# Linear-attention heads beside matrix products: keys stacked on the chip, scores a chunk ahead, wider decay steps

## The chip, the cores and the metric

The kernel runs on one core of a Trainium2 chip. Its time is the device time of one launch in microseconds (us), as the median of several runs. A core has five engines with instruction queues of their own, each in order: TensorE (PE, matrix products and transposes), VectorE (DVE), ScalarE (ACT), GpSimd (POOL) and SyncE (SP). SP and POOL issue the DMAs here.

## The reference, cut to what matters

A streaming encoder step with two layers, stick-breaking attention first and gated linear attention (GLA) second, for 512 prompt frames and 8 running streams of 16 new frames each (640 rows, width 2048). The change lies mostly in the GLA layer, which has 4 heads with 256 key and 512 value columns:

```python
def gla_chunk(S, inp):
    """S_t = diag(a_t) S_{t-1} + k_t^T v_t, o_t = q_t S_t; g = log a_t."""
    q, k, v, g = inp
    b = jnp.cumsum(g, axis=1)
    b_last = b[:, -1]
    q_in = q * jnp.exp(b)
    a = jnp.einsum('bchd,bshd->bhcs', q_in, k * jnp.exp(-b))
    a = jnp.where(jnp.tril(jnp.ones((C, C), dtype=bool)), a, 0.0)
    o = jnp.einsum('bhcs,bshe->bche', a, v) + jnp.einsum('bchd,bhde->bche', q_in, S)
    S = jnp.exp(b_last)[..., None] * S + jnp.einsum('bshd,bshe->bhde', k * jnp.exp(b_last[:, None] - b), v)
    return S, o
...
    g = log_sigmoid(a_lr @ w_a2 + b_a) / GLA_TAU          # the decays
    S, o = lax.scan(gla_chunk, S0, ...)
    o = o * lax.rsqrt(jnp.mean(o * o, axis=-1, keepdims=True) + EPS) * g_out
    y = (o * silu(r)) @ w_out
```

The prompt starts from a state of zeros; each of the 8 streams has a state of its own, read from and written to DRAM (256 x 512 numbers a head and stream).

## The kernel before, in words

Products keep nearly full precision with 32-bit operands split into a high and a low part (`halves`: a cast on ACT, a subtraction on DVE) and three products for one. The first 957 us hold the modulation (`six`) and the projections of layer 0 by seven products where eight would do (`by_sevens`); then the attention of layer 0 with plain and shared products beside it, up to 1538 us; queries and the seven-products of layer 1, up to 2072 us. Then comes the stage that the change is about, the heads' stage, to 2496 us, and the final products (L356 and L1746).

In the heads' stage PE works on a stream of large products, the fill: first `others` (L1314), the projections of q and k of heads 2 and 3 by `plain` (320 columns each, L575), then `share` for two groups of output rows (512 columns, L619). Between pieces of the fill the planner `Side` slips in steps of four lanes. A lane is a generator; `yield step(wait, tp, z)` says after how much of PE's work, on the planner's own count `pe["now"]`, its next step may come, and how many PSUM banks it takes. This fixes the order on PE. The instructions of the other engines follow from the code by a scheduler, and each engine's queue is in order.

- `decays` (L1396) makes a head's decays: the products of `alr_in` and `wa` (L1423), then ACT and DVE over 640 columns (Abs, Exp, Ln, a scan at L1429), and scales q and k in place by exponentials (L1445, L1446) by halves of the 640 columns, for the two halves `dt` of the 256 key columns. `wa` comes from six small loads `wa2r`. Heads 2 and 3 wait for all of `others`.
- `prompt_lane` (L1450) goes through 4 heads of 4 chunks: scores (`attend`, L1356), keys transposed (L1499) into `krh` and `krl`, the state as `S1h` and `S1l` (L1471, L1472), the output by `mm3` (L1344), `normed` (L1364, with a reciprocal root `on_r` on POOL at L230), and the state's update (L1525, L1527). `leave` (L1384) transposes the normalised rows (L1388), multiplies by the gate (L1389) and stores them as `og`; the gate of a later chunk is loaded into that buffer afterwards.
- `sample_lane` (L1556) does the 8 streams, 4 at a time in four groups a head (`e` for which of two streams, `dt`). A group multiplies the queries `qz` by four states (L1612, into the bank `z`), then updates each state by a product of the stacked keys `kst` and values `vst` (L1618) and DVE (L1620), and the state is stored (`leaves`) and, 8 us of PE work later, the next one asked into its buffer (`ask`). There are `S0` = 8 such buffers. `kst` holds high, high and low rows of the keys of four streams. They get there through DRAM: two transposes (L1584), `krh` and `krl` stored to `st_d`, and six loads for each `stack(e, dt)`, all on POOL's queue:

```python
def stack(e, dt):
    for i in range(3):
        rows = st_d[h][int(i == 2)][:, P * dt:P * dt + P].rearrange("(m e t) n -> e t m n", m=4, e=2)[e]
        r0 = 64 * e + NT * i
        move(kst[e][r0:r0 + NT].bitcast(F32), rows)
```

- `fetches` (L1630) loads rows `kt` of `og` (two buffers, tag `pl`, which the projections use too) and splits them into `ogh` and `ogl` for the fill. `share` starts when the four rows of its group are there (`side.until`, L1670). Rows 14 and 15 are loaded in the final stage.

Of the kernel before, what the change touches and what calls it, by code (L numbers as in the profile page):

```python
# [15 lines left out]
P = 128  # L16
# [17 lines left out]
S0 = 8  # L34
# [7 lines left out]
def hybrid_step_kernel(ctx: ExitStack, tc: tile.TileContext, A: dict, O: list):  # L42
# [77 lines left out]
    st_d = [[dp.tile([P, 256], F32, name=f"k_{h}_{d}") for d in range(2)] for h in range(GH)]  # L120
# [33 lines left out]

    def wpiece(src, a, n):

        return [t.rearrange("p (a n) -> p a n", a=a) for t in split(wraw(src, a, n))]
# [276 lines left out]
    def six(h, w, n0, acc, until, asked):  # L434
# [4 lines left out]
        def piece(j):  # L439
            asked()  # L440
            return wpiece(src[:, j:j + 9:8, n0:n0 + 512], 2, 512)

        nxt = piece(0)
        yield
        for j in range(8):
            until(j)
            wh, wl = nxt
            if j < 7:
                nxt = piece(j + 1)
# [107 lines left out]
    def plain(h, src, parts):  # L557
# [3 lines left out]
        def piece(n):  # L561
            if n < len(todo):
                n0, k0, _ = todo[n]
                return wpiece(src[:, k0:k0 + 8, n0:n0 + P], 8, P)

        nxt, acc = piece(0), None
        for n, (n0, k0, leave) in enumerate(todo):
# [3 lines left out]
            for nt in range(2):  # L571
# [33 lines left out]
    def share(g, og, w, leave=None, at=None, first=None):  # L605
# [30 lines left out]
        for c in range(4):  # L636
            ws = [w0, w1]
            if c < 3:
                raws += [raw(c + 1, 0), raw(c + 1, 1)]
                w0 = made()  # L640
# [3 lines left out]
            for a in each:  # L644
# [3 lines left out]
                leave(a, c, acc)  # L648
            if len(each) == 3:
# [648 lines left out]
    with tc.tile_pool(name="gl", bufs=1, reuse_waits="tile") as gl:  # L1298
        came = {"plain": False, "last": False}

        def keep(dst, hh):
            t = []

            def leave(nt, pt):
# [4 lines left out]
                if nt:  # L1309
                    move(dst[:, hh, :], t[0])  # L1310
            return leave
# [3 lines left out]
                                 for n0, dst in ((256 * h, gq_d[h]), (NK + 256 * h, gk_d[h])) for hh in range(2)])  # L1315
# [35 lines left out]
        def attend(t0, kT, qT):  # L1351
# [8 lines left out]
            parts = [gl.tile([P, P], F32R, tag=n, name=n, bufs=2) for n in ("aTh", "aTl")]  # L1360
# [3 lines left out]
        def normed(o):  # L1364
# [4 lines left out]
            r = rstd_of(gl, s1, 512, "on")  # L1369
# [26 lines left out]
        def decays():  # L1396

            for h in range(GH):
                while min(through.values()) < h - 1 or h >= 2 and not came["plain"]:
                    yield step(0.5)  # L1400
                q, k = (gl.tile([P, 2, T], F32, tag=n, name=n, bufs=2) for n in ("q", "k"))
                r = gl.tile([96, 256], F32, tag="e", name="wa2r", bufs=1)
                for n in range(6):
                    load(r[16 * n:16 * n + 16, :], A["gla_w_a2"][0][:, 256 * h:256 * h + 256])
                load(q, gq_d[h])
                load(k, gk_d[h])
# [3 lines left out]
                dve.tensor_tensor(wa2[64:96, :], r[64:96, :], wa2[64:96, :].bitcast(F32), op=ALU.subtract)  # L1410

                e1, el, ed = (gl.tile([P, 2, 4], F32, tag=n, name=n, bufs=2) for n in ("e1", "el", "ed"))
                es = gl.tile([P, 2, NB], F32, tag="es", name="es", bufs=2)
                yield step(5.0)
                for dt in range(2):
# [3 lines left out]
                    for c in hs:  # L1419
# [5 lines left out]
                        dve.tensor_scalar(y[:, c], pt, ba, 0.0, op0=ALU.add, op1=ALU.min)  # L1425
                    act(b, b, AF.Exp, scale=-1.0)
                    act(b, b, AF.Ln, bias=1.0)
                    dve.tensor_tensor(y, y, b, op=ALU.subtract)
                    dve.tensor_tensor_scan(b, reset, y, 0.0, ALU.mult, ALU.add)  # L1429
                    bp = b[:, :NP].rearrange("p (c t) -> p c t", t=P)  # L1430
# [6 lines left out]
                    act(ed[:, dt], ed[:, dt], AF.Exp, scale=IT)  # L1437
                    act(es[:, dt], bs[:, :, 15:16].rearrange("p c o -> p (c o)"), AF.Exp, scale=IT)
                    m = gl.tile([P, 4], F32, tag="m", name="m")
                    dve.tensor_copy(m, b1)  # L1440
                    dve.tensor_tensor(bp, bp, m.unsqueeze(2).to_broadcast([P, 4, P]), op=ALU.subtract)
                    for x, sign, f in ((q, 1.0, 1.0 / 16.0), (k, -1.0, 1.0)):
# [7 lines left out]
        def prompt_lane():  # L1450
# [25 lines left out]
            def leave_left():  # L1476
# [3 lines left out]
                if c == 3:  # L1480
                    through["p"] = h + 1
# [293 lines left out]
```

## Time and profile before

| | us |
|---|---|
| median of 3 runs | 2615.43 (2614.98 to 2615.93) |
| the profiled execution | 2618.87, span 2617.2 |
| PE busy in the span | 2448.4 (94%) |
| DVE, ACT, POOL busy | 1601.5, 1021.0, 259.5 |
| mean granted clock of PE | 0.971 of full speed |

The profile is of one execution. An engine's busy time is the time in which one of its instructions ran; a row of the trace gives an instruction's start and length, and in brackets how long the engine had been idle and what released it. Matrix products are pipelined: a product of 320 columns shows some 0.31 us, while the next one starts after about half of that. The granted clock is the share of full speed that PE was given, 1.00 for 2.4 GHz. A wait "issue" is one for which the profile shows no releaser.

### The profile page before, as it was taken

To read this page: it belongs to the slowest core of one execution; us is meant where nothing else is said; L and a number is where in the kernel's file an instruction comes from. 1 tells how busy PE (TensorE), PEld (TensorE's weight loads), DVE (VectorE), ACT (ScalarE), POOL (GpSimd) and SP (SyncE) were. 2 spreads that over 40 slices of the span, in tenths; PEclk is the share of its full clock that TensorE was granted. 3 is DMA by queue.
4 is the path that set the end of the run, shared out by engine and by line. 5 is a ranking of instruction groups with operands and counts; after the bars stand their busy time and mean duration, and the time that the engine had idled before them with its cause. 6 is when DMAs were issued, how large, how long until landed. Compare 5 with 4: busy or idle time off the path is not lost.

```text
span 2617.2 us, 43380 instructions
## 1 busy us (share of the span) xinstructions
PE 2448.4 (94%) x17169; PEld 2144.5 (82%) x17169; DVE 1601.5 (61%) x2436; ACT 1021.0 (39%) x1819; POOL 259.5 (10%) x537
## 2 busy tenths in 40 slices
PE   6889999999999989999999979999999997797998
PEld 3569999999999988787777768999999977575776
DVE  5555556555656645766776676666667564555556
ACT  4332222222223335565443354333333462463333
POOL 1210000000000000000000051000000234434300
PEclk7899999999999999999999989999999999898999
DMA  9966666766674366666665643334443577846564
GB/s 356 290 206 213 218 217 201 231 215 215 200 238 144 119 208 215 223 221 204 216 217 177 188 119 120 98 113 136 132 120 104 187 228 225 268 162 210 201 197 149
DMA packets 486813, 503.80 MB, mean 193 GB/s; under 512 B 25738, under 2 KB 408082, under 8 KB 486482
## 3 DMA queue, kind: packets, MB, share of 16 engines
q1 hardware_dynamic: 466578, 443.87, 53.8%
q0 software_dynamic: 17728, 54.54, 6.3%
q8 instruction: 135, 2.21, 0.3%
q10 hardware_dynamic: 2304, 2.62, 0.3%
q14 instruction: 68, 0.56, 0.1%
HBM read 411.16 MB, written 89.78 MB: 191 GB/s over the span
## 4 chain that ended last, share of the span: by engine, by line
PE 73%; DMA 9%; DVE 7%; issue 4%; ACT 3%; POOL 2%; SPq 1%; ACTq 0%; POOLq 0%; DVEq 0%
PE ps_mm L520 40%; PE ps_mm L619 8%; PE ps_mm L454 4%; PE ps_mm L356 3%; PE ps_mm L575 3%; PE ps_tp L975 2%; PE ps_z L178 1%; DMA ar<-in_w_ada_dram 1%; DVE wl L136 1%; PE ps_tp L943 1%; PE ps_z L919 1%; PE ps_z L218 1%; PE ps_tp L1020 1%; PE ps_mm L1746 1%; PE ps_tp L1344 1%
## 5 line engine op out<-in xcount | busy, mean ns | idle before, releaser
L520 PE MATMUL ps_mm<-sums,wh 128*128 128x320 f32 x2880 | 642.1, 311 | 0.0
L520 PE MATMUL ps_mm<-h,wh 128*128 128x320 f32 x2160 | 485.7, 313 | 14.1 <-ACT wh L135 13.1
L520 PEld LDWEIGHTS ps_mm<-sums,wh 128*128 128x128 f32 x2880 | 479.4, 188 | 11.5 <-issue 9.5
L520 PE MATMUL ps_mm<-sums,wl 128*128 128x320 f32 x1440 | 445.1, 309 | 0.1
L520 PEld LDWEIGHTS ps_mm<-h,wh 128*128 128x128 f32 x2160 | 361.0, 189 | 30.8 <-ACT wh L135 19.2
L136 DVE TENSOR_TENSOR wl<-wr,wh 128x1024 fp32r<-128x1024 f32 x191 | 234.9, 1231 | 228.1 <-ACT wh L135 226.9
L135 ACT CAST wh<-wb 128x1024 fp32r<-128x1024 f32 x180 | 189.5, 1053 | 462.6 <-PE ps_mm L520 370.0
L520 PE MATMUL ps_mm<-h,wl 128*128 128x320 f32 x1080 | 335.2, 310 | 1.1 <-DVE wl L136 1.1
L135 ACT CAST wh<-wr 128x1024 fp32r<-128x1024 f32 x191 | 200.5, 1051 | 305.7 <-PE ps_mm L520 198.0
L520 PEld LDWEIGHTS ps_mm<-sums,wl 128*128 128x128 f32 x1440 | 270.3, 188 | 0.3 <-DVE wl L136 0.3
L136 DVE TENSOR_TENSOR wl<-wb,wh 128x1024 fp32r<-128x1024 f32 x180 | 219.9, 1222 | 74.0 <-ACT wh L135 73.6
L619 PE MATMUL ps_mm<-wh,ogh 128*128 128x512 f32 x450 | 199.1, 442 | 15.0 <-ACT ogh L135 11.7
L575 PE MATMUL ps_mm<-h,wh 128*128 128x320 f32 x896 | 207.0, 318 | 3.3 <-DVE out L526 2.1
L520 PEld LDWEIGHTS ps_mm<-h,wl 128*128 128x128 f32 x1080 | 203.9, 189 | 1.7 <-DVE wl L136 1.7
L619 PE MATMUL ps_mm<-wh,ogl 128*128 128x512 f32 x450 | 180.4, 401 | 0.6 <-DVE ogl L136 0.5
L619 PE MATMUL ps_mm<-wl,ogh 128*128 128x512 f32 x450 | 180.3, 401 | 0.0
L575 PEld LDWEIGHTS ps_mm<-h,wh 128*128 128x128 f32 x896 | 150.8, 190 | 15.6 <-issue 10.9
L575 PE MATMUL ps_mm<-h,wl 128*128 128x320 f32 x448 | 139.5, 311 | 3.8 <-DVE wl L136 3.8
L619 PEld LDWEIGHTS ps_mm<-wh,ogh 128*128 128x128 f32 x450 | 87.5, 195 | 41.2 <-ACT ogh L135 12.8
L454 PE MATMUL ps_mm<-wh,h 128*128 128x512 f32 x288 | 102.0, 420 | 11.1 <-ACT h L135 8.0
L857 DVE TENSOR_TENSOR_SCAN k<-k,zero_c 128x544 f32<-128x544 f32 (+4 forms) x96 | 93.3, 975 | 29.9 <-ACT k L853 17.7
L619 PEld LDWEIGHTS ps_mm<-wh,ogl 128*128 128x128 f32 x450 | 86.5, 192 | 21.7 <-DVE ogl L136 1.8
(307 smaller groups left out, 3874.9 us busy)
## 6 DMA issues: line engine op xcount, KB each, us to landing
ar<-in_w_ada_dram SPq DMA_DIRECT2D x176, 512.0 KB
wb<-in_sb_w_in_dram SPq DMA_DIRECT2D x84, 512.0 KB
kc<-in_cache_sb_k_dram SPq DMA_DIRECT2D x64, 512.0 KB
vc<-in_cache_sb_v_dram SPq DMA_DIRECT2D x64, 512.0 KB
wb<-in_gla_w_in_dram SPq DMA_DIRECT2D x51, 512.0 KB
wr<-in_gla_w_in_dram SPq DMA_DIRECT2D x45, 512.0 KB
wr<-in_sb_w_in_dram SPq DMA_DIRECT2D x44, 512.0 KB
wr<-in_sb_w_out_dram SPq DMA_DIRECT2D x32, 512.0 KB
```

The costliest lines, as they stand in the source:

```text
L135: nc.scalar.copy(hi, x)
L136: dve.tensor_tensor(lo, x, hi.bitcast(F32), op=ALU.subtract)
L178: mm(acc[32 * q:32 * q + 32, :w], cT[:, kt + m, :], by(cT[:, kt + m, :], rs[m // each][:, m % each, q, :]), start=kt + m == 0, stop=kt + m ...
L218: mm(acc[32 * j:32 * j + 32, :256], cT[:, kt + m, :], by(cT[:, kt + m, :], r[:, 256 * j:256 * j + 256]), start=kt + m == 0, stop=kt + m == ...
L356: mm(acc[a], l[:, c], by(l[:, c], r[:, k2, :]), start=kt == k0 and first, stop=kt == k0 + nk - 1 and last)
L454: mm(acc[a], l, by(l, r[:, e, :]), start=j == 0 and e == 0 and first, stop=j == 7 and e == 1 and last)
L520: mm(acc, l[:, k, :], by(l[:, k, :], r), start=start and k == 0 and first, stop=k == 7 and last, skip_group_check=True)
L575: mm(acc[nt], l[:, k, :], by(l[:, k, :], r), start=k0 == 8 and k == 0 and first, stop=k0 == 0 and k == 7 and last)
L619: mm(acc, l, by(l, r[:, e, :]), start=i == 0 and e == 0 and first, stop=i == 1 and e == 1 and last)
L857: dve.tensor_tensor_scan(kr, kr, zeros[:, :w], 1.0, ALU.mult, ALU.add)
L919: mm(z[:, :n], q[:, hh, qs], by(q[:, hh, qs], k[:, hh, :n]), start=True, stop=True)
L975: turn_block(tp[:, P * c:P * c + P], block(kc[:, c, P * hh:P * hh + P]), ident)
```

## The change

- `st_d` and its stores and loads go. `stack(dt)` builds, for a half of the streams at a time, a tile `kc` of high, high, low, low keys by an ACT copy and a DVE subtraction from `kd`, transposes it on PE (two transposes for each of two halves and two `dt`, 8 a head where there were 2), and copies the result from PSUM into `kst` by ACT (`e` 0) and DVE (`e` 1).
- `S0` is 7; a state is asked 7 us after its store, which is issued 1.0 after the update.
- The prompt lane makes the scores and transposed keys of the next chunk before the output of this one (`scores(u + 1)`); the first state update comes before the second half of the output; `normed` is split into the sum of squares and `scaled_by`, which comes after the second update.
- `decays` scales by exponentials of 640 columns into `y`, in shorter steps; the weights of the next head are fetched ahead; heads 2 and 3 wait for their own projections only (`came["of"]`).
- The values of the sample lane are fetched for the next head when a head is done.
- `fetches` makes rows 0 to 9; rows 10 to 15 are loaded (six buffers) and split in the final stage.
- `plain` and `six` load their weight pieces one further ahead; `share` makes its next weight behind the first row block.

The diff, cut to its core:

```diff
-S0 = 8
+S0 = 7
...
-    def plain(h, src, parts):
+    def plain(h, src, parts, upper=None):
...
-        nxt, acc = piece(0), None
+        nxt, raw, acc = wsplit(piece(0), 8), piece(1), None
...
-                if nt == 0:
-                    nxt = piece(n + 1)
+                if nt == 0 and raw is not None:
+                    nxt, raw = wsplit(raw, 8), piece(n + 2)
                 if k0 == 0:
                     leave(nt, acc[nt])
+            if upper is not None and n == len(todo) - 2:
+                upper()
...
             if c < 3:
                 raws += [raw(c + 1, 0), raw(c + 1, 1)]
-                w0 = made()
...
                 leave(a, c, acc)
+                if a == each[0] and c < 3:
+                    w0 = made()
...
-            r = rstd_of(gl, s1, 512, "on")
+            return on, rstd_of(gl, s1, 512, "on"), o
+
+        def scaled_by(on, r, o):
             act(on, o, AF.Copy, scale=r)
             return on
...
+            wa2 = yield from weights(0)
             for h in range(GH):
-                while min(through.values()) < h - 1 or h >= 2 and not came["plain"]:
+                while min(through.values()) < h - 1 or h >= 2 and came["of"] < h:
                     yield step(0.5)
...
-                yield step(5.0)
+                yield step(1.0)
...
                     for x, sign, f in ((q, 1.0, 1.0 / 16.0), (k, -1.0, 1.0)):
-                        for c in hs:
-                            e = gl.tile([P, HALF], F32, tag="e", name="e", bufs=1)
-                            act(e, b[:, c], AF.Exp, scale=sign * IT)
-                            dve.scalar_tensor_tensor(x[:, dt, c], x[:, dt, c], f, e, op0=ALU.mult, op1=ALU.mult)
-                    yield step(10.0)
+                        act(y, b, AF.Exp, scale=sign * IT)
+                        yield step(0.8)
+                        dve.scalar_tensor_tensor(x[:, dt], x[:, dt], f, y, op0=ALU.mult, op1=ALU.mult)
                 ready[h] = q, k, e1, el, ed, es
+                if h + 1 < GH:
+                    wa2 = yield from weights(h + 1)
...
+                if u + 1 < len(units) and units[u + 1][0] in ready:
+                    yield step(0.3, tp=2)
+                    made = scores(u + 1)
+                yield step(1.8, tp=1)
...
+                yield step(0.3, tp=1)
+                update(0)
+                if c:
+                    yield step(1.5)
+                    mm3(o, [x[:, 1, :] for x in qc], s1, False, True)
+                if left is not None:
+                    yield step(0.3, tp=1)
+                    leave_left()
+                on = normed(o)
+                yield step(0.3, tp=1)
+                update(1)
...
+                left = u, scaled_by(*on)
...
-            side.after(8.0, ask)
+            side.after(7.0, ask)
...
-                khl = [gl.tile([P, 256], F32R, tag=n, name=n, bufs=2) for n in ("krh", "krl")]
-                halves(*khl, tp[:, :256])
-                for t, x in zip(st_d[h], khl):
-                    move(t, x.bitcast(F32))
...
+                def stack(dt):
+                    for half in range(2):
+                        x = gl.tile([P, 256], F32R, tag="kc", name="kc", bufs=1)
+                        x4 = x.rearrange("p (s i t) -> p s i t", s=4, i=4)
+                        kx = kd[:, dt, 64 * half:64 * half + 64].rearrange("p (s t) -> p s t", s=4).unsqueeze(2)
+                        kx = kx.to_broadcast([P, 4, 2, NT])
+                        nc.scalar.copy(x4[:, :, 0:2], kx)
+                        dve.tensor_tensor(x4[:, :, 2:4], kx, x4[:, :, 0:2].bitcast(F32), op=ALU.subtract)
+                        yield step(1.5, tp=1 - half)
+                        tp = tp if half else bank("tp")
+                        for m in range(2):
+                            c = P * (2 * half + m)
+                            turn_block(tp[:, c:c + P], block(x.bitcast(F32)[:, P * m:P * m + P]), ident)
+                    for e in range(2):
+                        r = slice(64 * e, 64 * e + 48)
+                        (dve.tensor_copy if e else nc.scalar.copy)(kst[e][r], tp[r].rearrange("p (m n) -> p m n", m=4))
...
-            for kt in range(14):
+            for kt in range(10):
...
-                    yield step(2.0)
+                    yield step(5.0)
                     ask_rows(kt)
-                    if kt % 4 < 3 and kt < 13 and came["plain"]:
+                    if kt % 4 < 3 and kt < 9 and came["plain"]:
                         ask_rows(kt + 1)
...
-        for kt in (14, 15):
-            r = po.tile([P, T], F32, tag="rows", name="og_in", bufs=2)
+        for kt in range(10, 16):
+            r = po.tile([P, T], F32, tag="rows", name="og_in", bufs=6)
```

How it moves instructions, at three places.

POOL's queue at the sample lane of head 0, before: the keys' stores (`k_0`, `k_1`), their loads into `kst`, then the chunk's gated rows (`og`), the first state's store and the next gate.

```order
L230 TENSOR_TENSOR on_r<-on_ms,mhalf 128x1
L78 DMA k_0_86<-krh 128x256
L78 DMA k_1_87<-krl 128x256
L78 DMA kst_21030<-k_0_86 16x4x128 x2
L78 DMA kst_21031<-k_0_86 16x4x128 x2
L78 DMA kst_21030<-k_1_87 16x4x128
L78 DMA kst_21031<-k_1_87 16x4x128
L78 DMA og_99<-gate 512x1x128
L78 DMA out_dram<-s_21044 128x512
L78 DMA gate<-gr_111 128x4x128
L78 DMA out_dram<-s_21046 128x512
```

Now:

```order
L232 TENSOR_TENSOR on_r<-on_ms,mhalf 128x1
L78 DMA out_dram<-s_21038 128x512
L232 TENSOR_TENSOR on_r<-on_ms,mhalf 128x1
L78 DMA og_91<-gate 512x1x128
L78 DMA out_dram<-s_21040 128x512
L78 DMA s_21777<-in_state_gla_dram 128x512
L78 DMA out_dram<-s_21042 128x512
L78 DMA gate<-gr_103 128x4x128
```

The stores and loads of the keys are gone, and the load of the eighth state (`s_21777`, into the buffer of the first) stands behind two stores, ahead of the gate load; the second group of products takes that state.

PE around the first state update of the prompt in head 0, before: `v,krh` and `v,krl` are the update's products, `ident,kd` the transposes of the sample keys, `q,k` scores.

```order
L1344 MATMUL ps_tp<-v,aTl 128x512
L575 MATMUL ps_mm<-h,wh 128x320 x2
L575 MATMUL ps_mm<-h,wl 128x320
L575 MATMUL ps_mm<-h,wh 128x320 x2
L575 MATMUL ps_mm<-h,wl 128x320
L1344 MATMUL ps_tp<-v,krh 128x512 x2
L1344 MATMUL ps_tp<-v,krl 128x512
L1584 MATMUL ps_tp<-ident,kd 128x128 x2
L575 MATMUL ps_mm<-h,wh 128x320 x2
```

Now (`ident,kc` are the transposes of the stacked keys):

```order
L1443 MATMUL ps_tp<-alr_in,wa_21397 128x320
L1355 MATMUL ps_tp<-v,aTh 128x512 x2
L1355 MATMUL ps_tp<-v,aTl 128x512
L1646 MATMUL ps_tp<-ident,kc 128x128 x2
L579 MATMUL ps_mm<-h,wh 128x320 x2
L579 MATMUL ps_mm<-h,wl 128x320
L579 MATMUL ps_mm<-h,wh 128x320 x2
L579 MATMUL ps_mm<-h,wl 128x320
L1355 MATMUL ps_tp<-v,krh 128x512 x2
L1355 MATMUL ps_tp<-v,krl 128x512
```

The stacked keys are transposed before the first update already, and the decays of the next head (`alr_in`) come ahead of the chunk's output. From the first `alr_in` product of head 0 to its first scores PE has 120 fill products where it had 174, and that first product stands 24 fill products earlier.

ACT in the decays of head 0, before: the exponentials of the first half of the key columns (`e<-b`), then the second half's start.

```order
L1438 ACTIVATE es<-b 128x8
L1437 ACTIVATE ed<-ed 128x4
L1445 ACTIVATE e<-b 128x320 x3
L135 CAST wh<-wr 128x1024
L1445 ACTIVATE e<-b 128x320
L1308 COPY pl<-ps_mm 128x320
L1424 ACTIVATE b<-ps_tp,cols 128x320 x2
```

Now:

```order
L1460 ACTIVATE es<-b 128x8
L1463 ACTIVATE ed<-ed 128x4
L1467 ACTIVATE y<-b 128x640 x2
L1444 ACTIVATE b<-ps_tp,cols 128x320 x2
L1447 ACTIVATE b<-b 128x640
L134 CAST wh<-wr 128x1024
L1640 CAST kc<-kd 128x4x32
```

Four exponentials of 320 columns have become two of 640, and the second half starts right behind them.

## Rows read from the trace of the kernel before

**Rows 1.** Busy time by stretches: us, engines busy (x instructions), granted clock, DMA share, GB/s

```profile
2072.00:2262.00 190.00, 168.72 (x1038) 147.84 (x1039) 100.14 (x178) 86.94 (x165) 82.06 (x147) 0.96 0.78 248
2262.00:2290.00 28.00, 10.27 (x39) 6.66 (x37) 14.05 (x27) 15.16 (x30) 6.71 (x11) 0.74 0.81 251
2290.00:2497.00 207.00, 181.14 (x814) 137.93 (x815) 117.82 (x207) 94.71 (x177) 72.64 (x125) 0.94 0.56 185
```

**Rows 2.** PE's waits, 2060 to 2515 us: in total, times, longest

```profile
PE ps_tp L1618 <- DMA kst<-k: 22.1, 3, 10.5
PE ps_mm L619 <- ACT ogh L135: 9.4, 2, 7.8
PE ps_tp L1388 <- ACT on L1370: 7.6, 5, 2.9
PE ps_z L1612 <- DMA s<-in_state_gla_dram: 7.4, 5, 3.3
PE ps_tp L1344 <- ACT S1h L1471: 7.2, 1, 7.2
...
PE ps_tp L1618 <- DVE s L1620: 2.0, 1, 2.0
PE ps_tp L1618 <- DVE gate L1389: 1.5, 1, 1.5
PE ps_mm L356 <- DVE gate L1389: 1.4, 1, 1.4
```

**Rows 3.** In order of time, one long gap: start, us, instruction, idle before

```profile
2206.89 0.76 POOL L78 DMA_DIRECT2D gate<-gr  x1 [3.69 <-issue]
...
2208.21 0.57 POOL L230 TENSOR_TENSOR on_r<-on_ms,mhalf 128x1 f32<-128x1 f32 x1
2208.73 2.08 POOL L78 DMA_DIRECT2D kst<-k  x4
...
2213.41 0.76 PE L1618 MATMUL ps_tp<-vst,kst 128*128 128x512 f32 x1 [10.47 <-DMA kst<-k]
...
2213.97 0.73 PE L575 MATMUL ps_mm<-h,wh 128*128 128x320 f32 x2
```

**Rows 4.** DMA issues, 2072 to 2497 us: KB each, median us to landing

```profile
out_dram<-s POOLq DMA_DIRECT2D x64, 256.0 KB, 3.5
s<-in_state_gla_dram POOLq DMA_DIRECT2D x63, 256.0 KB, 5.4
```

**Rows 5.** Groups of instructions, 2060 to 2500 us: busy us, mean ns, idle before

```profile
L1620 DVE SCALAR_TENSOR_TENSOR s<-s,es,ps_tp 128x512 f32<-128x512 f32 x64 | 46.9, 743 | 31.1 <-PE ps_tp L1618 29.2 <-DMA og<-gate 1.6
...
L78 POOL DMA_DIRECT2D out_dram<-s x64 | 35.5, 555 | 50.6 <-DVE s L1620 34.4 <-issue 5.9 <-DVE qcl L136 2.1
...
L1388 PE MATMUL ps_tp<-ident,on 128*128 128x128 f32 x80 | 13.2, 290 | 7.6 <-ACT on L1370 7.6
```

**Rows 6.** In order of time, the start of the heads' stage

```profile
2075.68 6.54 SPq L71 DMA_DIRECT2D wa2r<-in_gla_w_a_dram  x6
...
2086.67 0.41 PE L1423 MATMUL ps_tp<-alr_in,wa 96*128 96x320 f32 x1 [0.69 <-DVE wa L1410]
...
2099.38 0.32 PE L1423 MATMUL ps_tp<-alr_in,wa 96*128 96x320 f32 x1
2099.53 0.46 PE L575 MATMUL ps_mm<-h,wh 128*128 128x320 f32 x2
...
2114.07 0.49 DVE L1446 SCALAR_TENSOR_TENSOR k<-k,e 128x320 f32<-128x320 f32 x1 [0.54 <-ACT e L1445]
```

**Rows 7.** In order of time, the gap behind `others`

```profile
2274.48 0.73 ACT L135 CAST ogh<-og_in 128x640 fp32r<-128x640 f32 x1 [3.32 <-DMA og_in<-og]
...
2289.98 0.80 PE L619 MATMUL ps_mm<-wh,ogh 128*128 128x512 f32 x1 [7.80 <-ACT ogh L135]
```

**Rows 8.** Two stretches of 20 us, columns as in rows 1

```profile
2200.00:2220.00 20.00, 9.53 (x55) 7.37 (x54) 6.05 (x10) 3.00 (x6) 9.25 (x16) 0.74 0.65 210
...
2460.00:2480.00 20.00, 20.00 (x96) 16.36 (x95) 12.27 (x22) 6.83 (x12) 3.55 (x5) 1.00 0.28 93
```

More of the change, by code (lines that the diff above doesn't have):

```diff
@@ L1310, in leave @@
                     move(dst[:, hh, :], t[0])
+                    for h in (2, 3):
+                        if hh and dst is gk_d[h]:
+                            came.update(of=h, when=pe["now"])
             return leave
         others = plain(h2, src, [(n0 + P * hh, keep(dst, hh)) for h in (2, 3)
-                                 for n0, dst in ((256 * h, gq_d[h]), (NK + 256 * h, gk_d[h])) for hh in range(2)])
+                                 for n0, dst in ((256 * h, gq_d[h]), (NK + 256 * h, gk_d[h])) for hh in range(2)],
+                       lambda: came.update(plain=True))
         for _ in range(2):
@@ L1516, in prompt_lane, with update @@
                     s1 = state(S, e1, 1, c)
-                    yield step(3.0)
-                    mm3(o, [x[:, 1, :] for x in qc], s1, False, True)
-                left = u, normed(o)
-                for dt in range(2):
-                    yield step(0.3, tp=1)
+                def update(dt):
                     pt = bank("tp")
@@ L1565, in sample_lane @@
                         move(vst[r0:r0 + NT].bitcast(F32), rows)
+                return v, gate(h, NP, "gn", 1)
+            here = fetch(0)
+            for h in range(GH):
+                v, g = here
                 while h not in ready:
@@ L1598, in sample_lane @@
+                yield step(4.0)
+                yield from stack(0)
                 yield step(0.5, tp=1)
                 a = attend(NP, k, q)
-                yield step(5.0)
+                yield step(3.0)
                 o = bank("z")
                 mm3(o, a, v, True, False)
-                since = pe["now"] + 9.0
+                since = pe["now"] + 1.0
                 for n in range(4):
@@ L1608, in sample_lane @@
                         yield step(0.3)
-                    yield step(max(since, max(states[x][1] for x in group) + 7.0) - pe["now"], tiled=True)
+                    yield step(max(since, max(states[x][1] for x in group) + 8.0) - pe["now"], tiled=True)
                     for m in range(4):
@@ L1621, in sample_lane @@
                                                  op0=ALU.mult, op1=ALU.add)
-                        side.after(1.5, lambda x=group[m]: leaves(x))
-                    if n < 2:
-                        stack(e, 1)
+                        side.after(1.0, lambda x=group[m]: leaves(x))
+                    if n == 1:
+                        yield from stack(1)
+                        yield step(1.5)
                 on = normed(o)
-                yield step(8.0, tp=1)
+                on = scaled_by(*on)
+                yield step(7.0, tp=1)
                 leave(h, NP, on, g)
                 through["s"] = h + 1
+                if h + 1 < GH:
+                    yield step(4.0)
+                    here = fetch(h + 1)
         def fetches():
@@ L1655, in fetches @@
                 halves(*og1[kt], rows.pop(kt))
[L1656 removed]
+                if kt % 4 < 3 and kt < 9 and kt + 1 not in rows:
                     ask_rows(kt + 1)
```

110 lines of the change are left out of this document (58 added, 52 removed).

## The prediction

> **What bounds the kernel now.** I read the busy time by stretches first: the stage of the heads is the three stretches from 2072 to 2497 us, in which TensorE (PE) is busy 360.13 us of 425, while VectorE, ScalarE and GpSimd are each busy under 233 [rows 1]. So PE sets the time here, and what can be won is its idle time: 64.87 us. Next comes what ended it, the list of PE's waits [rows 2]. Four kinds carry it: the sample lane's state update waiting for the stacked keys' loads (22.1 us, three times); the products of the output stage waiting for `ogh`, and one chunk's product waiting for `S1h`, which both belong to the gap behind the last products of `others` (9.4 and 7.2); the transposes of normalised rows (7.6); and the products with the sample states (7.4). Shorter ones, from 2.0 us down, make up the rest. Then I read one long gap in order of time, to see what stands in front of the loads [rows 3].
>
> An effect of 0.2%, 5.2 us, is about what a measurement of this kernel can tell from no change.
>
> **The change, part by part.** The sum is made against the profiled execution's own 2618.87 us; the median of the runs shown is 2615.43, 3.4 us lower.
>
> *Stacked keys by transposes.* In [rows 3] the queue of GpSimd issues a gate load after 3.69 us in which it waited, then the small `on_r` and the first four `kst<-k`, one behind the other; PE starts the update only after 10.47 us idle. The change takes the 8 stores and 48 loads away and makes `kst` on the chip. The 22.1 us of [rows 2] go. PE pays 32 transposes instead of 8. The 80 of the normalised rows stand in groups of four and are busy 13.2 us, 0.66 a group, at 0.290 for one [rows 5]; a further one thus costs (0.66 - 0.29) / 3 = 0.12, and 24 cost +2.9 us (bounds 0, if all fall into waits, and 4.0 at 13.2 / 80 each). ACT's copy, DVE's subtraction and the two copies out of PSUM come twice a head and lie beside PE's other work, of which the order puts 5 us or more between the last of these transposes and the first update that needs them; without that cover the update would be late by four short instructions, below 3 us, since the wider cast in [rows 7] takes 0.73.
>
> *Seven state buffers.* The 7-buffer ring makes the fourth state of a group take the buffer of the first state of the group before. Its chain, from the first `kst` product to the next group's `z` products: product 0.4, update 0.743, store issue 0.555 and landing 3.5, load issue as much and landing 5.4 [rows 4, 5], which is 11.2 us. The order of the change leaves this chain PE work of 11.0, 14.2, 11.1; 12.2, 13.7, 9.9; 9.0, 13.7, 10.2; 9.2, 14.6, 9.3 us in the four heads (counted in its order, with products of 320 columns at 0.15 us from start to start [rows 6], those of 512 at 8/5 of that). The shortfalls add up to 8.7 us if the chain takes 11.2, to 12.2 at 11.7, to 22.1 at 13. I take 12.2, since a load that lands late costs more than an early one saves; before it was 7.4 [rows 2]: +4.8 (bounds -1 and +15). The Trainium skill ("DMA: Bandwidth & Descriptors", section "Anatomy of one DMA") gives a DMA about 2.0 us and its bytes over 436 GB/s, which for 256 KB is an estimate of 2.6 us. By that the chain would take 7.3 us, no group would wait, and the sum would be 12.2 us lower. [Rows 4] have 5.4 and 3.5 us for these loads and stores, and the row decides.
>
> *Decays in wider steps, the keys earlier.* ACT and DVE do the same columns in 16 instead of 32 instructions each, which is off the bound. The start moves: between the first `alr_in` product and the first scores PE had 174 fill products, now 120, with three more `alr_in` products 18.1 us. The chain beside them, from rows: the second half's `alr_in` at 2099.38 to the last scaled key at 2114.56 is 15.2 us [rows 6]; in the new order that half begins 9.1 us after the first, so the keys are there after 24.3, and PE waits 6.2 where it waited for nothing. The first `alr_in` also comes 24 fill products (3.5 us) earlier, but PE waited 0.69 us for `wa` already, whose loads SP issues at the same place of its queue [rows 6]: the wait becomes 4.2. Together +9.7 (bounds +2, if the halves overlap better than in the row, and +12).
>
> *Scores one chunk ahead, rows normalised later.* The rows that were waited for 7.6 us [rows 2] now have a chunk's scores and an update between normalisation and transposes: -6.1, leaving 1.5 (bounds -7.6 and 0). The waits of update products for `s` and `gate` (2.0 and 1.5), one each, stood at places that the new order changes: -2.0 (bounds -3.5 and 0). Against it, heads 2 and 3 start from decays that now end nearer to their first scores, +3 (0 to +5, the startup's wait over again).
>
> *The gap behind `others`.* From 2262 to 2290 PE is idle 17.7 us [rows 1]: rows of `og` go through two buffers shared with the projections, so ACT waits for each load, and PE for ACT [rows 7]. The change keeps the two buffers. But `upper` sets its flag before `others` ends, so two rows are asked at once instead of one after the other's conversion: two rounds of a load (5.4 us as for states [rows 4]) and two conversions (0.73 us on ACT [rows 7] and about as much on VectorE, each) come to 17 us instead of 28. The first row is asked 3 us of PE work later than before, and 7 us of the lanes' products stand in the gap. I take 10 us idle, -7.7 (bounds -13 and -1).
>
> *Rows 10 to 13 beside the final products.* Conversions leave the stage; their loads run while the first products of the final stage multiply. The 1.4 us for the last gate [rows 2] goes, as 36 products now stand behind the last leave: -1.4. Only rows 12 to 15 depend on the last leave; the 36 products and the 60 of rows 8 to 11 lie before them, 96 x 0.24 = 23 us, against a gate product, a store and a load, some 10 us by the states' rows [rows 4]. So it is covered; without cover the wait would be that 10.
>
> *Weight pieces one ahead* in `plain` and `six`: loads of 512 KB a piece earlier. In the first stage it lets one load pass another on SP's queue and adds none: 0, bounds -1.5 and +1.5.
>
> *The clock.* The granted clock is 0.74 in the 20 us with the gap of 10.47 and 1.00 in an undisturbed stretch [rows 8]. Right behind the gap a pair of 320-column products takes 0.73 us [rows 3] where it takes 0.46 [rows 6]; some 4 us at that pace lose about 2 us behind each long gap, an estimate. Four long gaps become two or three: -3 (bounds -8 and 0).
>
> *Waits that a new order makes* and no row can show: +2 (0 to +8).
>
> Sum: -22.1 +2.9 +4.8 +9.7 -6.1 -2.0 +3 -7.7 -1.4 -3 +2 = -19.9. The profiled execution would take 2599.0 us, the median of runs **2595.6 us**.
>
> **The rivals.**
> *Full gain.* The new waits are absorbed: decays of the first head overlap and startup adds 2 instead of 9.7, and the state loads land in time (no 12.2). For it: ACT is busy 197 us of the 425 [rows 1] and 56 DMAs of about 0.555 us [rows 5] leave GpSimd's queue, 31 us, so all others are issued earlier. Against it: 5.4 us landing is a median under this very load. That is another -19.9 us: 2575.7. The Trainium skill's estimate for one load, above, speaks for it too.
>
> *No change.* The loads were only the last of several things that the sample lane waited for. In [rows 3] the gate load in front waited 3.69 us and `on_r` was stuck behind it, and this stays: gates, stores and loads of states share the in-order queue. If the 22.1 us fall to 11 rather than 0, and the gap behind `others` stays, the sum is -19.9 + 11 + 7.7 = -1.2: 2614. It also covers that the change doesn't do what it says: stacked keys that PE gets no earlier, since `kd` waits for the decays.
>
> *Slower: the ring of seven states becomes the bound.* Mechanism: store and load of a state stand on GpSimd's queue, in order, behind gate loads that wait as the one in [rows 3]. If one such wait falls into each chain, it takes 3.69 us more, about 15.3, and every group but the first of a head waits: 12 x 15.3 - 138.1 (the sum of the twelve distances) = 45.5 us instead of 12.2, so -19.9 + 33.3 = +13.4: 2629. It decides from a chain of 14.2 us on, where the shortfalls of the distances above are 32.7 us and nothing is left of the gain. Against it: GpSimd has 31 us less to issue, and with 8 buffers PE waited only 7.4.
>
> **How the numbers follow.** Forecast 0.50, with its own range 2583 to 2607 (the bounds of startup, states and gap are 8, 10 and 6 us to a side; taken as independent they make some 12); full gain 0.18; no change 0.17; slower 0.15. Range for 8 in 10: 2576 to 2617; it leaves out the slower case and the lower half of the full gain. Faster by over 0.2% means under 2610.2: the forecast, the full gain and a small part of the third case, 0.69; within 0.2%, 0.16; slower, 0.15.
>
> **What would show it.** In the profile after: no `kst<-k`, and PE's update products wait under 3 us in total; PE idle in 2072 to the end of the stage about 45 us in place of 65; the first scores wait some 6 us and the first `alr_in` some 4; `z` products wait for `s` in 5 to 10 groups, 12 us together; the gap behind `others` about 10 us; the final products begin without a wait; the granted clock below 0.8 in at most two stretches of 20 us. It is wrong if `s` waits exceed 25 us, if the gap behind `others` is 15 us or more, or if any stage ahead of 2072 us differs by over 2 us.

## The result, and the profile after

The changed kernel takes 2597.63 us (median of 5 runs, 2594.68 to 2606.23) against 2615.93 (5 runs, 2614.98 to 2621.53): a ratio of 0.9923, with a 95% interval of 0.9906 to 0.9940. The forecast was 2595.6. The profiled execution of the changed kernel took 2595.40 us with a span of 2593.4. Its five runs lie up to 11.6 us apart, where the forecast took 5.2 us for the resolution, so differences under 5 us are not read below.

PE's waits of the changed kernel, the same view as [rows 2] with a window from 2040 to 2500 us (line, what it waited for, us in total, times, longest):

```profile
PE ps_tp L1367 <- DVE k L1469: 9.9, 2, 7.7
PE ps_tp L1402 <- ACT on L1384: 8.0, 3, 5.6
PE ps_z L1667 <- DMA s<-in_state_gla_dram: 4.5, 2, 3.0
PE ps_tp L1443 <- DMA v<-gv: 4.3, 1, 4.3
...
PE ps_tp L1646 <- DVE kc L1641: 2.7, 2, 2.2
PE ps_mm L625 <- ACT ogh L134: 2.4, 1, 2.4
PE ps_mm L358 <- DVE y L630: 2.4, 1, 2.4
...
PE ps_tp L1355 <- DVE kst L1649: 1.1, 1, 1.1
```

The waits for the keys' loads (22.1 us) are gone; `kst` and the tile `kc` it comes from cost 3.8 us. The products that use `kst` (L1673) never wait for it: the 1.1 us belong to a product of the prompt lane (L1355). All waits of this list together are 43.9 us, where those of before were 64.8. New are the first scores (L1367, for the last scaled key) and the first `alr_in` product (L1443; the profile names a load of `v`, but the product stands behind `wa`). The normalised rows are waited for as long as before, 8.0 us for 7.6.

The places in order of time, PE's timeline (start, us, instruction, idle before): the two at the start, those for states, the last product of `others` (L579 at 2277.23) and the long ones behind it:

```profile
2083.87 0.64 PE L1443 MATMUL ps_tp<-alr_in,wa 96*128 96x320 f32 x1 [4.26 <-DMA v<-gv]
2112.40 0.80 PE L1367 MATMUL ps_tp<-q,k 128*128 128x128 f32 x2 [7.72 <-DVE k L1469]
...
2183.78 1.63 PE L1667 MATMUL ps_z<-s,qz 128*32 128x512 f32 x2 [2.99 <-DMA s<-in_state_gla_dram]
...
2249.91 1.04 PE L1667 MATMUL ps_z<-s,qz 128*32 128x512 f32 x2 [1.50 <-DMA s<-in_state_gla_dram]
...
2277.23 0.31 PE L579 MATMUL ps_mm<-h,wl 128*128 128x320 f32 x1
...
2294.18 0.50 PE L625 MATMUL ps_mm<-wh,ogh 128*128 128x512 f32 x1 [2.43 <-ACT ogh L134]
2301.14 1.11 PE L1402 MATMUL ps_tp<-ident,on 128*128 128x128 f32 x4 [5.59 <-ACT on L1384]
...
2472.32 0.47 PE L358 MATMUL ps_mm<-wh,ogh 128*128 128x512 f32 x1 [2.36 <-DVE y L630]
```

The final products begin at 2472.32 us instead of 2496.10, 23.8 earlier, and the whole span is 23.8 shorter. Of this, 1.9 us come from ahead of the heads' stage, whose last preceding product starts at 2069.59 us instead of 2071.49. That is scatter: with the same code ahead of the stage, that product starts at 2066.2 us in e5 and at 2071.8 in e9. The stage itself is 21.9 us shorter, 402.7 us for 424.6, with 20.9 us less of waits and 0.9 us less of busy time.

The gap behind `others` has moved. `others` ended at 2262.2 us before and ends at 2277.5 now, so the stretch of 2262 to 2290 us, with 10.27 us of busy PE in [rows 1], still holds the last 15 us of `others` in the changed kernel. The gap is the second of these stretches (columns as in rows 1):

```profile
2262.00:2290.00 28.00, 26.19 (x149) 20.32 (x148) 21.56 (x40) 17.42 (x34) 12.59 (x24) 1.00 0.85 293
2277.50:2302.00 24.50, 14.53 (x65) 9.24 (x63) 12.61 (x23) 11.29 (x21) 10.83 (x21) 0.89 0.91 287
```

PE is idle 10.0 us there, where it was idle 17.7 us before.

The loads of the states land faster (DMA issues from 2072 to 2475 us, KB each, median us to landing), 4.3 us against the 5.4 of [rows 4]; the stores take the same:

```profile
out_dram<-s POOLq DMA_DIRECT2D x64, 256.0 KB, 3.5
s<-in_state_gla_dram POOLq DMA_DIRECT2D x59, 256.0 KB, 4.3
```

So the time came out as forecast. Whether the parts did is the question of the runs.

### The profile page after: what moved, and what is told of

Same layout as the page of the kernel before. It is cut to its first block, busy times and chain, and to the rows that moved or that the text cites. A ratio compares the mean times of both kernels' runs of the same rounds, so it can differ in the third digit from the quotient of the medians.

```text
span 2593.4 us, 43364 instructions
## 1 busy us (share of the span) xinstructions
PE 2449.4 (94%) x17193; PEld 2153.0 (83%) x17193; DVE 1608.4 (62%) x2440; ACT 1023.0 (39%) x1823; POOL 232.8 (9%) x481
## 4 chain that ended last, share of the span: by engine, by line
PE 77%; DVE 7%; DMA 6%; issue 4%; ACT 3%; POOL 2%; SPq 1%; POOLq 0%; ACTq 0%; DVEq 0%
PE ps_mm L524 42%; PE ps_mm L625 9%; PE ps_mm L458 4%; PE ps_mm L358 3%; PE ps_mm L579 3%; PE ps_tp L982 2%; PE ps_z L180 2%; PE ps_tp L950 1%; PE ps_z L926 1%; PE ps_z L220 1%; PE ps_tp L1027 1%; DVE wl L135 1%; PE ps_z L995 1%; PE ps_mm L1806 1%; DMA ar<-in_w_ada_dram 1%
## 5 line engine op out<-in xcount | busy, mean ns | idle before, releaser
L524 PE MATMUL ps_mm<-h,wh 128*128 128x320 f32 x2160 | 485.2, 313 | 14.1 <-ACT wh L134 12.9
L579 PE MATMUL ps_mm<-h,wh 128*128 128x320 f32 x896 | 210.4, 322 | 2.8 <-DVE out L530 2.4
L579 PEld LDWEIGHTS ps_mm<-h,wh 128*128 128x128 f32 x896 | 153.8, 194 | 14.6 <-issue 10.5
L579 PE MATMUL ps_mm<-h,wl 128*128 128x320 f32 x448 | 141.1, 315 | 2.2 <-DVE wl L135 2.2
```

Source lines behind the costliest of these rows:

```text
L524: mm(acc, l[:, k, :], by(l[:, k, :], r), start=start and k == 0 and first, stop=k == 7 and last, skip_group_check=True)
L579: mm(acc[nt], l[:, k, :], by(l[:, k, :], r), start=k0 == 8 and k == 0 and first, stop=k0 == 0 and k == 7 and last)
```

## The experiments

The theory was that of the prediction: the keys' loads were the gain, the start a loss, the gap behind `others` closed by asking two rows at once, the ring of states close to its bound. Each run's time is the median of 4 runs or more (e1: 10, e4: 8), its ratio is to the kernel before in the same session.

| kernel | median, us | ratio to before, 95% interval | PE's waits 2060 to 2515, us |
|---|---|---|---|
| before | 2614 to 2616 | 1 | 64.8 |
| the change | 2597.6 | 0.9923 [0.9906, 0.9940] | 43.9 |
| e1 change, keys through DRAM | 2611.9 | 0.9993 [0.9980, 1.0006] | 58.0 |
| e2 change, later start | 2597.4 | 0.9930 [0.9910, 0.9951] | 42.6 |
| e3 change, rows as before | 2594.7 | 0.9915 [0.9893, 0.9937] | 42.0 |
| e4 change, 6 state buffers | 2603.0 | 0.9954 [0.9940, 0.9968] | 44.8 |
| e5 before, stacked keys and 7 buffers | 2571.8 | 0.9828 [0.9808, 0.9847] | 27.2 |
| e6 change, scores not ahead | 2601.2 | 0.9945 [0.9924, 0.9967] | 48.0 |
| e7 change, gates on SP | 2585.2 | 0.9881 [0.9860, 0.9902] | 37.4 |
| e8 e2 and e7 together | 2593.6 | 0.9907 [0.9883, 0.9931] | 39.7 |
| e9 before, 7 buffers | 2600.9 | 0.9939 [0.9922, 0.9956] | 49.2 |
| e10 e5 with the new decays | 2590.0 | 0.9906 [0.9891, 0.9921] | 41.4 |
| e11 change, decays of before | 2588.1 | 0.9898 [0.9883, 0.9912] | 35.6 |
| e12 e5, gates on SP | 2586.1 | 0.9893 [0.9875, 0.9912] | 36.2 |

### e1: the keys through DRAM again

```diff
-                def stack(dt):
...
+                khl = [gl.tile([P, 256], F32R, tag="s" + n, name=n, bufs=1) for n in ("krh", "krl")]
+                halves(*khl, tp[:, :256])
+                for t, x in zip(st_d[h], khl):
+                    move(t, x.bitcast(F32))
+                def stack(e, dt):
...
```

`stack` is that of the kernel before, with its six loads from `st_d`.

> The change with the stacked keys through DRAM as before (two transposes a head, 8 stores, 48 loads on GpSimd's queue), all else as changed. Theory (the loads of the keys were what PE waited for, and their 22.1 us were won): 15 to 22 us above the change's 2597.6, so 2613 to 2620, with waits of the update products for `kst` of 12 us or more. Rival (the loads were only the last of several waits, and the gain comes from the scores a chunk ahead and the new order): 2598 to 2604, the waits for `kst` under 5 us.

Measured 2611.9, 14 us above the change. The waits are back in full (PE's waits of e1):

```profile
PE ps_tp L1671 <- DMA kst<-k: 17.4, 2, 9.6
PE ps_tp L1368 <- DVE k L1470: 8.5, 1, 8.5
PE ps_tp L1671 <- issue: 8.3, 1, 8.3
```

They are 25.7 us in three waits of the update products (the profile puts one of them down to no releaser). The rival falls: the keys were the last thing waited for. The time moves 14 us, just short of the theory's 15 to 22 and less than the waits, since other waits of PE are shorter here; all of them together are 14.1 us more than in the change.

### e2: the start later

```diff
-                yield step(1.0)
+                yield step(1.0 if h else 5.0)
...
+                if h == 0:
+                    yield step(7.0)
                 ready[h] = q, k, e1, el, ed, es
```

> The change with head 0's decays placed 4 us of PE work later and its first scores 7 us later. Theory (the two waits at the start, 4.3 for the first `alr_in` and 7.7 for the first scores, are plain losses): both waits under 1.5 us each, 7 to 12 us below the change, 2586 to 2591. Rival (the lanes' length sets the end, so that what is not waited for at the start is waited for behind): the start's waits go, the time stays at 2595 to 2600.

Measured 2597.4, no change, and the rival holds: 0.5 us is left of the 12.0 at the start, but PE waits as long in all. In its place stand (PE's waits of e2):

```profile
PE ps_z L1669 <- DMA s<-in_state_gla_dram: 9.8, 2, 6.8
PE ps_tp L1402 <- ACT on L1384: 8.3, 3, 4.1
PE ps_tp L1443 <- ACT on L1384: 6.7, 1, 6.7
PE ps_mm L579 <- ACT pl L1315: 5.0, 1, 5.0
```

They stand later in the stage, from 2106 us on: the steps behind the moved one have moved too, and land on other waits.

### e3: the rows of `og` as before

```diff
-            for kt in range(10):
+            for kt in range(14):
...
-                    yield step(5.0)
+                    yield step(2.0)
...
-        for kt in range(10, 16):
+        for kt in (14, 15):
```

with the flag set after `others` as before.

> The change with the fetches of `og` rows as before: rows 0 to 13 in the stage, the first asked 2 us after its turn, one at a time until `others` has ended. Theory (the gap behind `others` closed because two rows are asked at once and conversions are fewer): idle of PE between 2255 and 2300 us back to 12 to 18 us, 2607 to 2614. Rival (it closed because the lanes' products stand there now): 2596 to 2602.

Measured 2594.7, not slower than the change; the theory falls. PE is idle 5.3 us between 2255 and 2300 us, but that window says little, as `others` ends at 2284.7 us in e3. In the 24.5 us behind its end PE is idle 7.8 us, against 10.0 in the change, so the gap shrinks without any edit of the rows. In the changed kernel itself SP's timeline shows that in the gap no two rows are asked at once:

```profile
2266.95 0.32 SPq L71 DMA_DIRECT2D og_in<-og  x1
2275.98 0.32 SPq L71 DMA_DIRECT2D og_in<-og  x1
2282.06 0.32 SPq L71 DMA_DIRECT2D og_in<-og  x1
2286.69 0.32 SPq L71 DMA_DIRECT2D og_in<-og  x1
```

In the first 10 us of the gap the changed kernel has products of the lanes, with 1.8 us of waits, where before one product waited 7.2 us for `S1h`. The seven buffers alone (e9) leave 10.3 us idle in the 24.5 us behind the end of `others` there, about as little as the whole change. So the rival's reading fits, but it is the order as a whole that closes the gap, and no run isolates which step does.

### e4: six state buffers

```diff
-S0 = 7
+S0 = 6
```

> The change with 6 state buffers. The prediction's ring (a chain of 11.7 us, store and load of a state behind each other): with 6 the third and fourth state of a group depend on the group before, PE waits for `s` by 15 to 30 us, 2612 to 2627. Rival (loads land in 4.1 us since the keys' DMAs are gone, so the ring has slack): waits for `s` under 10 us, and 2599 to 2606, from the lanes ending some 8 us of PE work later.

Measured 2603.0; PE waits 2.2 us for states. The rival holds. The planner asks for a group's `z` products only 8 us of PE work after its last state has been asked, so fewer buffers move the groups apart instead of making PE wait: a head's groups start 15.6 us apart on average, in the change 14.7. Its reason ("since the keys' DMAs are gone") was wrong: in e1, with these DMAs, the loads land in 4.3 us too.

### e5: the stacked keys alone

The kernel before with `S0 = 7`, `st_d` removed, and `stack(dt)` of the change.

> The kernel before with the stacked keys by transposes alone, and 7 state buffers, since 8 leave no room for the new tile. Theory (the waits for the keys' loads carry most of the gain, and the rest of the change gives and takes about as much): waits of the update products under 4 us, 12 to 18 us below the kernel before, 2598 to 2604. Rival (the keys pay only together with the new order): 2609 to 2615. If s loads land in about 4.3 us as in the change, fewer buffers in flight are what made them faster.

Measured 2571.8, 43 us below the kernel before and 26 below the change, far under the theory's 2598. PE waits 27.2 us in all (PE's waits of e5):

```profile
PE ps_tp L1593 <- DVE kc L1588: 6.9, 3, 4.3
PE ps_z L1614 <- DMA s<-in_state_gla_dram: 5.1, 3, 3.3
PE ps_tp L1387 <- ACT on L1369: 4.2, 2, 3.0
PE ps_mm L618 <- ACT ogh L134: 3.6, 2, 2.7
...
PE ps_tp L1422 <- DVE wa L1409: 0.4, 1, 0.4
```

The start costs 0.4 us, and `ogh` is waited for 3.6. The condition in the expectation's last sentence is not met: the loads of states land in 5.0 us here, with 7 buffers. So the other parts of the change together lose 26 us in the presence of this one. That raised two questions, which part loses, and whether the 7 buffers have a share; e9 to e11 answer them.

### e6: scores not ahead

```diff
-                if u + 1 < len(units) and units[u + 1][0] in ready:
+                if False:
```

> The change without the scores of the next chunk ahead: a chunk's scores and transposed keys come at its own start, 2 us before its output. Theory (little of the gain is from this part): within 4 us of the change, 2594 to 2602. Rival (the scores ahead hide ACT's and DVE's work of each chunk): waits of the prompt's products for `aTh`, `aTl`, `krl` of 8 us or more in all, 2604 to 2612.

Measured 2601.2, within 4 us of the change: the theory holds. (Its profiled execution took 2607.2, the slowest of the four.) PE's waits for `aNh`, `aTl`, `S1h` and `S1l` (and `aNl`, `aTh`) grow to 15.8 us from 2.5 in the change; those for the normalised rows shrink to 5.4.

### e7 and e8: gates off GpSimd's queue

```diff
-            move(g, gr_d[h][:, :, t0:t0 + P])
+            load(g, gr_d[h][:, :, t0:t0 + P])
...
-            move(og_d[h][:, :, t0:t0 + P], g)
+            store(og_d[h][:, :, t0:t0 + P], g)
```

> The change with the loads of the gates and the stores of `og` on SP's queue instead of GpSimd's (40 DMAs). Theory (what is left of PE's idle time comes through GpSimd's queue, where the reciprocal root and the states stand behind gate loads that wait): ACT's waits for `on_r` from 17.5 to under 6 us, PE's for normalised rows from 8.0 to under 3, 5 to 10 us below the change, 2588 to 2593. Rival (SP then waits in the same way ahead of the weights' and rows' loads): 2596 to 2606, with waits of ACT for `wr` or `og_in` 10 us longer.

> The later start of e2 and the gates on SP of e7 together. Theory (e2's gain at the start was lost again to waits behind GpSimd's queue): both waits of the start under 1.5 us and those for normalised rows and states under 6 us together, 10 to 17 us below the change, 2581 to 2588. Rival (the lanes' own length is the bound): no lower than the better of e2 and e7, 2594 or more.

e7 takes 2585.2, a little more than the theory's gain: PE's wait for normalised rows falls from 8.0 to 1.3 us, ACT's for `on_r` from 17.5 to 9.0, not under 6. e8 takes 2593.6, above e7; its rival holds. What e2 and e7 win does not add up.

### e9: seven buffers alone

```diff
-S0 = 8
+S0 = 7
```

> The kernel before with 7 state buffers and nothing else. Theory (e5's 43 us come from the stacked keys): waits for `kst` stay above 18 us, 2612 to 2622. Rival (with 7 buffers the planner spreads the four groups of a head evenly, and that alone was much of e5's gain): 2590 to 2604, with waits for `kst` under 12 us.

Measured 2600.9, 13 us below the kernel before. The rival's time holds, though its waits don't: those for `kst` are all there. What has shrunk are the waits for `S1h`, from 7.2 to 0.9, and half of those for states (PE's waits of e9):

```profile
PE ps_tp L1618 <- DMA kst<-k: 22.8, 3, 8.5
PE ps_mm L619 <- ACT ogh L135: 8.0, 2, 4.9
PE ps_tp L1388 <- ACT on L1370: 7.9, 1, 7.9
PE ps_z L1612 <- DMA s<-in_state_gla_dram: 3.8, 1, 3.8
```

and the loads of states land in 4.3 us, with 8 buffers in 5.4. The order tells the difference: with 8 buffers the states of two groups are there together, and from the first group's `z` products to the second's PE is busy only 6 to 9 us, to the third's another 11 to 18; with 7 it is 9 to 19 us between any two groups of a head. That the spacing is the cause is argued, not shown; no run kept 8 buffers and spread the groups.

### e10 and e11: the decays

e10 puts the change's `decays` into e5; e11 puts the `decays` of before into the change.

> e5 (stacked keys, 7 buffers) with the change's decays: 640 columns at once, shorter steps, weights ahead, heads 2 and 3 on their own projections. Theory (the decays' earlier start is what costs in the change): waits of 3 to 5 us for the first `alr_in` and 6 to 9 for the first scores come back, 2582 to 2590. Rival (the cost lies in the prompt lane, the rows or the raw pieces): 2569 to 2576.

> The change with the decays of the kernel before, all else as changed. Theory (as e10): no wait over 1.5 us at the start, 10 to 17 us below the change, 2581 to 2588. Rival (as e2 had it: what isn't waited for at the start is waited for behind): 2594 to 2601.

Both theories hold, e11's at the edge of its range: 2590.0, 18 us above e5, and 2588.1, 9.5 below the change, with 1.6 us of waits left at the start. In e10 the start's waits are back, and the normalised rows' are doubled (PE's waits of e10):

```profile
PE ps_tp L1390 <- ACT on L1372: 8.5, 3, 5.9
PE ps_mm L618 <- ACT ogh L134: 5.5, 1, 5.5
PE ps_tp L1358 <- DVE k L1457: 5.1, 1, 5.1
PE ps_tp L1431 <- DVE wa L1407: 4.4, 1, 4.4
```

With e5 and the change this is a square of two edits: from e5, the new decays cost 18.2 us and the remaining parts (prompt lane, rows, raw pieces) 16.3, both together 25.8. The stage lengths of the profiled executions agree: 379.1 us in e5, 397.2 in e10, 395.4 in e11, 402.7 in the change. Added up, the two would cost 34.5 us, 8.7 more than together, with intervals of 4 to 5 us to a side of each kernel's time. So the decays' edit is a loss either way. e2 did not show it, since it moved only the start and kept the new steps, the weights fetched ahead and the earlier decays of heads 2 and 3; which of those carries the rest is open.

### e12: the stacked keys alone, gates on SP

e5 with the diff of e7.

> e5 with the gates' loads and the stores of `og` on SP's queue, as in e7. Theory (GpSimd's queue is what is left; e7 won 12 us by it): waits for `kc`, `s` and normalised rows from 16.2 to under 10 us, 2560 to 2567. Rival (e7 won by where its waits happened to fall, since with e2's start the same edit won 4): 2569 to 2578.

Measured 2586.1, 14 us above e5: outside both, on the far side of the rival. The edit that won 12 us in the change loses 14 in e5. PE waits 12.2 us for `kc` (6.9 in e5) and 7.8 for `y`, and SP now has waits of the gates' DMAs (waits of SP in e12, from 2060 to 2500 us):

```profile
SPq L71 <- DMA og<-gate: 56.6, 17, 8.0
...
SPq L74 <- DVE gate L1388: 33.1, 11, 6.4
```

These totals don't explain the loss, since e7 has more of them, 44.9 and 69.1 us, and gains. What explains it is what they hold up. The 7.8 us for `y`, in order of time (timelines of SP, ACT and PE in e12):

```profile
2292.11 1.58 SPq L71 DMA_DIRECT2D wa2r<-in_gla_w_a_dram  x3
2301.30 0.53 SPq L71 DMA_DIRECT2D gate<-gr  x1
2301.87 1.75 SPq L71 DMA_DIRECT2D wa2r<-in_gla_w_a_dram  x3
...
2306.20 0.40 ACT L1408 CAST wa<-wa2r 96x256 fp32r<-96x256 f32 x1 [12.86 <-DMA wa2r<-in_gla_w_a_dram]
...
2308.66 0.79 PE L618 MATMUL ps_mm<-wh,ogh 128*128 128x512 f32 x1 [7.78 <-ACT y L626]
```

A gate load waits in SP's queue between the third and the fourth of the six loads of weights, ACT waits 12.86 us for these, and the copy of `y` stands behind that on ACT. The 7.5 us for `kc` go the same way: ACT waits 14.56 us for rows `og_in`, which SP issues behind a gate load. So here the rival that e7 named happens. Whether e7's own gain came from GpSimd's queue or from where its waits happened to fall is not settled.

## Why the prediction was right, and where its steps were not

The time was right: 2597.6 for 2595.6, PE idle 43.4 us from 2072 us to the end of the stage for the 45 forecast. Several terms are near what was measured, and the errors of the others cancel: buffers -7.7 us, keys +3.8, tail +2.4, start +1.6. That they cancel is luck.

- **Stacked keys** (-22.1, and 2.9 for the transposes): the mechanism was right and e1 shows it. The waits fell by 22.1 - 3.8 = 18.3 us; the cover of PE work held for the products that use `kst`, but not for the transposes, which wait 2.7 us for `kc`. The price in time inside the change is 14 us (e1).
- **Seven state buffers** (+4.8): the sign was wrong. The waits for states fell from 7.4 to 4.5, and e9 gives 13 us of gain to this edit alone. The chain was counted with a load that lands in 5.4 us; in the change it takes 4.3. By the same sum that is a chain of about 10.1 us and shortfalls of 0.2 + 1.1 + 0.9 + 0.8 = 3.0 us (distances 9.9, 9.0, 9.2 and 9.3), near the 4.5 measured, but not at the places: the two waits, 2.99 and 1.50 us, stand at distances of 11.1 and 12.2 us, and none at the four short ones. So the sum of distances is not what sets them. Ahead of the first wait the chain runs into a gate load on GpSimd's queue, which is the mechanism of the slower rival, once instead of in every group (GpSimd's timeline of the change):

```profile
2173.53 0.78 POOL L78 DMA_DIRECT2D gate<-gr  x1 [4.42 <-DMA og<-gate]
2174.30 0.55 POOL L78 DMA_DIRECT2D out_dram<-s  x1
...
2179.43 0.54 POOL L78 DMA_DIRECT2D s<-in_state_gla_dram  x1
```

The landing time was read from a kernel whose order the edit changes. The Trainium skill ("DMA: Bandwidth & Descriptors", "Anatomy of one DMA") gives such a load an estimate of 2.6 us. No run shows it: the lowest median for these loads is 4.2 us (e2 and e7). With that estimate the prediction's chain comes to 7.5 us, not the 7.3 written, and still no group would wait.
- **The start** (+9.7): right in place and near in size. 4.26 us for the first `alr_in` (forecast 4.2) and 7.72 for the first scores (forecast 6.2), worked out from the order's distances and the rows' chain. e10 and e11 show that the decays' edit, which brings it, is a loss, e2 that taking the start's waits away by themselves wins nothing.
- **Scores ahead, rows normalised later** (-6.1, -2.0, +3): the last two came out, as the update products' waits for `s` and `gate` fell from 3.5 to 1.4 us and the first scores of a later head wait 2.1. The first did not: the normalised rows are waited for 8.0 us, not 1.5. Of these, 5.59 are one wait in the gap behind `others`, and 2.4 are elsewhere. In the gap PE waits for ACT, ACT 4.23 us for `on_r` on GpSimd, and `on_r` stood behind a store of `og` that waited 3.85 us (timelines of GpSimd and ACT in the change):

```profile
2299.05 0.73 POOL L78 DMA_DIRECT2D og<-gate  x1 [3.85 <-issue]
2299.72 0.64 POOL L232 TENSOR_TENSOR on_r<-on_ms,mhalf 128x1 f32<-128x1 f32 x1
...
2300.39 0.69 ACT L1384 ACTIVATE on<-ps_tp,on_r 128x512 f32<-128x512 f32 x1 [4.23 <-POOL on_r L232]
```

More PE work between two steps does not help where the step itself is stuck in a queue. The prediction named this queue for its rivals and did not draw it into this term.
- **The gap behind `others`** (-7.7): right in size, 10.0 us idle for the 10 forecast with the wait of 5.59 in it, but not for the stated reason. Two rows are not asked at once, and the gap is as small with the rows as before (e3) and with the seven buffers alone (e9). Of what is left only 2.4 us are for `ogh`.
- **The tail** (-1.4): 2.4 us at the first final product, now for `y` (L630), so +1.0.
- **The clock** (-3): one stretch of 20 us in the heads' stage is below 0.8 (0.74 at 2300 to 2320), where the forecast allowed two; before there were three. PE's busy time in the stage falls by 0.9 us although 24 transposes have come to it.
- The rival of the full gain missed too: its way (no wait at the start, no wait for states) is not what e5 does to get under 2575. The rival of no change needed 11 us of waits for `kst` and the old gap, and had neither. The rival of the slower ring fell with e4 and e9.

What the method lacks in general: the sum treated each edit as a price to be added to the order of before. The square of e5, e10, e11 and the change (18.2 and 16.3 apart, 25.8 together) and e7 against e12 (-12 and +14 for the same diff) show that prices of reordering edits do not add here.

The fastest kernel measured is e5, stacked keys and 7 buffers only, 2571.8 us: 26 us below the change.

## What to carry to other kernels

Take DMA round trips out of a dependent chain first, and run that edit alone before anything is added to it: here it was worth more by itself than with its company, 29 us from e9 to e5 and 14 from e1 to the change. In a program whose order a planner fixes, PE's waits summed over the stage are a better measure of an edit than the one wait that it removes, because a removed wait often turns up at the next step. And a tile count is an edit of the order too: fewer buffers can be faster.

## What the runs showed of the hardware that was not expected

- With one state buffer less and nothing else changed (e9), the median load of 256 KB on GpSimd's queue landed in 4.3 us instead of 5.4. In the other kernels with 7 buffers it took 4.2 to 5.0 us (5.0 in e5), so the number of buffers is not all that sets it.
- Time falls faster than PE's waits do. In the profiled executions the heads' stage takes 424.6 us in the kernel before and 379.1 in e5, 45.5 less, while the waits fall by 37.6. The rest is PE's busy time in the stage, 359.5 us and 351.7, at a mean granted clock of 0.94 and 0.98 (the stage before, then in e5, columns as in rows 1):

```profile
2071.49:2496.10 424.61, 359.54 (x1888) 291.70 (x1886) 232.27 (x412) 197.12 (x371) 160.78 (x281) 0.94 0.68 218
...
2066.18:2445.30 379.12, 351.73 (x1911) 290.07 (x1909) 237.33 (x432) 201.82 (x391) 131.66 (x225) 0.98 0.73 237
```

In e5 no stretch of 20 us in the stage is below 0.83.
